# Due times in a list scheduler, and three GpSimd operations moved to VectorE, in a streaming-encoder layer

## The chip, the cores and the metric

The kernel runs on one core of a Trainium2 chip. The metric is the device time of one execution in microseconds (us). A core has engines with instruction queues of their own: TensorE (PE; its weight loads are listed as PEld), VectorE (DVE), ScalarE (ACT), GpSimd (POOL), and SyncE (SP), which issues most of the DMA transfers. Each engine executes its queue in order; a semaphore makes an instruction wait for another engine or for a transfer, and what stands behind it on the same queue waits with it.

## The reference

One layer of a streaming encoder is applied to a prompt of 2048 frames and to 8 running streams of 16 new frames each (the "sample"), with shared weights. Cut to what matters:

```python
h = rms_norm(x, norm_g)
z = einsum("btd,de->bte", h, w_in)                 # 1024 -> 3584 columns
u_a, v_a, g_a, q, k, v, g_b = split(z)             # 512 columns each
y_a = u_a * spatial_gate(v_a, ...) * silu(g_a)     # 4 groups x 128, W_s lower-triangular in 128-chunks
q, k = rms_norm(q), rms_norm(k)                    # per 64-wide half, 4 heads x 2 halves
# per head: two score maps; ALiBi distance; block-causal mask for the prompt
s = q @ k.T / 8 - slope[h] * abs(q_pos - k_pos)
a = softmax(s[half 0]) - lam * softmax(s[half 1])
o = rms_norm(a @ v, subln_g) * (1 - lam_init)
y_b = o * silu(g_b)
y = x + concat(y_a, y_b) @ w_out
```

For the sample, keys and values are the 1024 cached frames of each stream followed by its 16 new ones. Besides y, the new keys and values and the sample's `v_a` are outputs.

## The kernel before

**Number form.** All products are in fp32r. An operand that needs more precision is held as two parts: the high part is a rounded copy (`act.copy` on ACT), the low part is source minus high part. `split` does both; its argument `lo_eng` chooses the engine of the low part (DVE unless POOL is named). `mm3` multiplies two split operands with three matmuls. Every matmul is recorded on line 394 and every transpose on line 398, so tiles tell them apart; `split` has ACT on line 459 and the low part on line 460.

**Stages.**

1. *Projection* (`p1_pools`, `stream`). Tiles of 128 frames are normalized and transposed (`x_tp`, `xT`). Blocks of 256 columns of `w_in` are loaded in eight pieces (`load_w`: `wraw` by SP, scaled on ACT into `w`'s high part on line 626, the low part on DVE on line 627), and `project` accumulates `acc`. The kinds of block are `qk`, `v`, `ug` (gate and u) and `vg` (v and gate). `vg_group` normalizes `v_a` (`vn`, line 724; `vhl`), and makes the attention's gate: `gate` gives `sg` on DVE (line 690), and line 715 multiplies it by the constant `subg` into `gb`, which goes to the scratch `g_scr`.
2. *Sample attention*, woven into the projection. `sample_scores` loads cached keys (`skraw`), transposes and splits them (`skT`), and multiplies them with a block-diagonal query (`qbd`) into `sS`. Of `sS`, one half of the partitions is copied by ACT into `slo` (line 1104), line 1105 adds the distance `dist_s` to it, and DVE adds the other half and takes the running maximum into `sp` (line 1106). `sample_values` loads values (`svraw`, a ring of two buffers), splits them into `sv` (ring of two; low part on POOL), and accumulates `sO`.
3. *Prompt attention*. Frames 0 to 1023 (`attention_a`) are woven into the projection; 1024 to 2047 into the output projection. `score_steps` makes `S` and the exponentials `ex` (lines 889, 893, 905, 908, 909), `value_steps` transposes them (`a_tp`, `aT`) and accumulates `oT`. Values (`v_chunk`) are split with the low part on POOL.
4. *Output projection* (`out_stream`): `y_tp`, `yT`, `oo`, and the sum with x in `xo`.

**The order.** `weave` lays out program order: it takes steps of two generators in turn by estimated TensorE time. Then `Order(tc).run()`, a list scheduler of the kernel's own, fixes the order of each engine's queue. It replays the whole program on a clock. An instruction becomes ready when all those that it depends on have ended by that clock (`cost` gives to each a time to its result and a time that it holds its engine; `reach` and `SLACK`/`OTHER` are added for a result that goes to another engine; a transfer takes `FETCH` ns and more), and its buffers are free. For two-operand DVE work and POOL work, which `port` marks, it also keeps DVE and POOL out of each other's way. Whenever an engine is free, it takes among the ready instructions the one that comes first in program order:

```python
heapq.heappush((turn if port[i] else now_)[e], i)
...
i = heapq.heappop(turn[e])
```

SP's transfers are put in order the same way. The result is tied down as same-engine dependencies; on the chip the queues then run by semaphores alone.

Of the kernel before, what the change touches and what calls it, by code (L numbers as in the profile page):

```python
# [16 lines left out]
ALU = mybir.AluOpType  # L17
# [42 lines left out]
class Order:  # L60
# [4 lines left out]
    PE, ACT, DVE, POOL, SP = (mybir.EngineType.PE, mybir.EngineType.Activation, mybir.EngineType.DVE,  # L65
                              mybir.EngineType.Pool, mybir.EngineType.SP)

    SLACK = {PE: 180.0, SP: 300.0}
    OTHER, FETCH = 50.0, 2300.0

    class Node:
        def __init__(self, ins, idx):
# [115 lines left out]
    def cost(self, n):  # L188

        kind = type(n.ins).__name__[4:]  # L190
        size = max([math.prod([k for s, k in a.ap[1:]]) for a in n.reads + n.writes] or [1])
        accum = len(n.writes) > 1
        if n.dma:
            return 0.0, 560.0 if n.engine == self.POOL else 400.0
        if n.engine == self.PE:
            size = math.prod([k for s, k in n.writes[0].ap[1:]])
            t = 109.0 if size <= P else 4 + 0.4455 * size
            return t + 165, t
        if n.engine == self.ACT:
            t = 165 + 0.83 * size if kind == "TensorCopy" else 205 + 0.835 * size  # L200
            return (t + 190, t + 90) if accum else (t, t - 105)
        if n.engine == self.DVE:
            t = {"TensorTensor": 160 + 1.04 * size, "TensorReduce": 160 + 1.03 * size, "Memset": 100 + 0.5 * size,
                 "Reciprocal": 162.0}.get(kind, 205 + 1.04 * size)
            if size == 1:
                return (270.0, 190.0) if kind == "TensorScalarPtr" else (165.0, 90.0)
            if kind == "TensorScalarPtr" and not n.ins.is_scalar_tensor_tensor:
                t = 170 + 0.56 * size
            return (t + 100, t - 40) if accum else (t, t - 85)
        if kind == "Memset":  # L210
            return 100 + 0.83 * size, 100 + 0.83 * size
        if "pow" in str(n.ins):
            return 300 + 200.0 * size, 250 + 200.0 * size
        t = 190 + 2.16 * size if kind == "TensorTensor" else 195 + 1.1 * size
        return t, t - 50

    def port(self, n):

# [7 lines left out]
        large = math.prod([k for s, k in n.writes[0].ap[1:]]) >= 512 and type(n.ins).__name__ == "InstTensorScalarPtr"  # L226
        return int(len(wide) > 1 or (len(wide) == 1 and large and not psum))

    def run(self):
        N = self.nodes  # L230
        reach = {self.PE: 54.0, self.POOL: 80.0, self.SP: 27.0}
        for n in N:
            n.wait = len(n.deps)
            for d in n.deps:
                N[d].after.append(n.idx)
# [17 lines left out]
        for g in self.gates:  # L253
            for i in g[1]:
                gate[i].append(g)
            for i in g[2]:
                N[i].wait += 1
        cost = [self.cost(n) for n in N]
        ready = [0.0] * len(N)
        left = {k: len(q) for k, q in self.queue.items()}  # L260
        users = {x: len(self.uses[x]) for x in self.tag}
# [51 lines left out]
        while left_over:  # L313
            t, e = None, None
            for x in free:
                lock = busy[2 if x == self.DVE else 1]
                for y in ((free[x],) if now_[x] else ()) + ((max(free[x], lock),) if turn[x] else ()) + (
                        (max(free[x], later[x][0][0]),) if later[x] else ()):
                    if t is None or y < t:
                        t, e = y, x  # L320
            while later[e] and later[e][0][0] <= t:
                i = heapq.heappop(later[e])[1]
                heapq.heappush((turn if port[i] else now_)[e], i)
            lock = busy[2 if e == self.DVE else 1]
            if turn[e] and lock <= t and (not now_[e] or turn[e][0] < now_[e][0]):
                i = heapq.heappop(turn[e])
            elif now_[e]:
                i = heapq.heappop(now_[e])
            else:
                continue  # L330
            left_over -= 1
            n = N[i]
            out[e].append(i)
            if n.dma:
                size = 4 * math.prod([k for s, k in n.writes[0].ap])
                dma = max(t + self.FETCH, dma) + max(size / 280, 60.0)
                end = dma + 200
            else:
                end = t + cost[i][0]
            free[e] = t + cost[i][1]  # L340
            if port[i]:
                busy[port[i]] = free[e]
            for j in n.after:
                b = N[j].engine
                if b == e and not n.dma and not N[j].dma:
                    r = free[e]
                else:
                    r = end + reach.get(b, 35.0) + (self.SLACK.get(b, self.OTHER) if b != e or n.dma else 0)
                ready[j] = max(ready[j], r)
                N[j].wait -= 1  # L350
                if not N[j].wait:
                    arrive(j)
            more = list(first[i])
            for g in gate[i]:
                g[0] -= 1
                if not g[0]:
                    more += g[2]
            for j in more:
                ready[j] = max(ready[j], t)
                N[j].wait -= 1  # L360
                if not N[j].wait:
                    arrive(j)
            for name in n.tiles:
                if name in users:
                    last[name] = max(last.get(name, 0.0), end + 35)
                    users[name] -= 1
                    if not users[name]:
                        taken.discard(slot[name])
                        freed[slot[name]] = last[name]
            while held and place():  # L370
                pass
# [7 lines left out]
def trunk_step_kernel(  # L379
# [97 lines left out]
    turn = {}  # L477
# [30 lines left out]
    def p1_pools(stage, at):  # L508
# [194 lines left out]
        def vg_group(h, tiles, w, loads):  # L703
# [5 lines left out]
            for k, (pr, load) in enumerate(zip(pairs(tiles), loads)):  # L709
                m = len(pr)  # L710
                acc = yield from project(pr, w, load)
                va = sbg.tile([P, 2, P], F32, name="va", tag="va")[:, :m]
                act.copy(va, acc[:, :, 0])
                s = gate(acc, m)
                pool.tensor_tensor(out=gb[:, 2 * k:2 * k + m], in0=s,  # L715
                                   in1=subg.unsqueeze(1).broadcast_to([P, m, P]), op=ALU.mult)
                if sample:
                    sp.dma_start(nsg[:, h * P:(h + 1) * P], va[:, 0])
                st = sb.tile([P, 2, 2], F32, name="vst", tag="vst")
                for i in range(m):  # L720
                    act.activation(vn[:, 2 * k + i], va[:, i], AF.Square, scale=ISQ128, accum_out=st[:, 0, i:i + 1])
                rstd(st[:, 1, :m], st[:, 0, :m])
                for i in range(m):
                    dve.scalar_tensor_tensor(out=vn[:, 2 * k + i], in0=va[:, i], scalar=st[:, 1, i:i + 1],
                                             in1=sgug[:, h], op0=ALU.mult, op1=ALU.mult)
# [333 lines left out]
    def sample_scores(sa, b, qkT, qbd, dist_s, res):  # L1059
# [12 lines left out]
        for u in units:  # L1072
# [19 lines left out]
            if pend:  # L1092
                ci_, h_, kT_, w_ = pend
                s = bank("sS", "sS")[:, :w_]
                for i in range(2):
                    g = h_ + i
                    for z in range(2):
                        pe.matmul(s, lhsT=qbd[:, g * P:(g + 1) * P], rhs=kT_[:, z, i, :w_],
                                  start=i == 0 and z == 0, stop=i == 1 and z == 1)
                cost += pe_time(4 * w_)  # L1100
                hp, x = h_ // 2, 256 * ci_
                rh, rl = [slice(64 * k, 64 * k + 64) for k in (hp, 1 - hp)]
                lo = los[rh, ci_ % 2, :w_]
                act.copy(lo, s[rl])  # L1104
                pool.tensor_tensor(out=lo, in0=lo, in1=dist_s[rh, x:x + w_], op=ALU.add)  # L1105
                dve.tensor_tensor_reduce(out=p[rh, x:x + w_], in0=s[rh], in1=lo, scale=1.0, scalar=prev[hp],
                                         op0=ALU.add, op1=ALU.max, accum_out=st[rh, ci_:ci_ + 1])
                prev[hp] = st[rh, ci_:ci_ + 1]
# [16 lines left out]
    def sample_values(sa, b, a):  # L1125
        bs = slice(b * QS, (b + 1) * QS)

        def load(kt):
            n = P if kt < 8 else QS
            raw = sa.tile([P, 512], F32, name="svraw", tag="svraw")[0:n]  # L1130
            sp.dma_start(raw, cv[b, kt * P:(kt + 1) * P] if kt < 8 else nvs[bs].rearrange("t h d -> t (h d)"))
            v = sa.tile([P, 2, 512], F32R, name="sv", tag="sv")[0:n]
            split(raw, v[:, 0], v[:, 1], pool)
            return v

        vs = [load(0), load(1)]
# [76 lines left out]
    with ExitStack() as left, ExitStack() as right:  # L1213
# [108 lines left out]
        x = 0  # L1322
# [63 lines left out]
```

## Time and profile before

| | |
|---|---|
| median of 3 runs | 1396.93 us (1396.93 to 1399.89) |
| the profiled execution | 1396.8 us, span 1395.0 us |
| granted TensorE clock, mean | 0.998 |
| busy share PE / PEld / DVE / ACT / POOL | 97 / 90 / 64 / 57 / 44 % |
| matmuls | 9892 |
| PE busy in the slice 0 to 50 us | 36.65 us |
| POOL, low part of `sv` (72 instructions) | 94.4 us |
| POOL, `slo` plus distance (64) | 50.0 us |
| POOL, `gb` (36) | 26.6 us |

A row of the groups gives the line, engine, operation, tiles written and read, shape and count; then busy time in us and the mean of one in ns; then the engine's idle time just before those instructions, and what ended it. In a row of a tile, the three numbers are minimum, median and maximum duration in ns. Overlapping records make busy time smaller than count times mean.

### The profile page before, as it was taken

How to read it: one execution, taken by the hardware profiler on the slowest of the kernel's cores; microseconds unless marked ns; L12 is line 12 of the kernel's file. 1: busy time of each engine (PE TensorE's matmuls, PEld its weight loads, DVE VectorE, ACT ScalarE, POOL GpSimd, SP SyncE). 2: the span in 40 equal slices, each digit the busy share in tenths (PEclk: the TensorE clock that was granted, in tenths of full speed). 3: DMA queues.
4: the chain of work that ended last, by engine and by line, in shares of the span. 5: the costliest groups of instructions: out<-in, count | busy, mean ns of one | idle time of the engine just before them, and what ended most of it. 6: DMA issues, size and time to landing. Idle time of an engine off the chain costs nothing. (4 is left out here: it accounts for less than half of the span.)

```text
span 1395.0 us, 27945 instructions
## 1 busy us (share of the span) xinstructions
PE 1355.2 (97%) x9892; PEld 1258.4 (90%) x9892; DVE 889.4 (64%) x2114; ACT 794.0 (57%) x1778; POOL 615.9 (44%) x796
## 2 busy tenths in 40 slices
PE   6999999999999999999999999999999999999998
PEld 5999999999999899999999999997788888888887
DVE  4433447765666684798887764324888887877721
ACT  5433347766565776677656553224676777676620
POOL 2261534646464565656625142023555545445400
PEclk9999999999999999999999999999999999999999
DMA  6623234544545576645533242235555444442323
GB/s 196 191 82 112 71 89 144 158 140 131 144 125 154 151 205 193 180 126 130 159 92 110 74 145 81 79 120 190 157 150 166 129 120 127 148 125 65 103 84 102
DMA packets 209244, 183.05 MB, mean 131 GB/s; under 512 B 21104, under 2 KB 167024, under 8 KB 209104
## 3 DMA queue, kind: packets, MB, share of 16 engines
q1 hardware_dynamic: 199280, 155.17, 37.9%
q0 software_dynamic: 9824, 26.09, 6.8%
q8 instruction: 78, 1.28, 0.4%
q14 instruction: 62, 0.51, 0.1%
HBM read 130.86 MB, written 42.47 MB: 124 GB/s over the span
## 5 line engine op out<-in xcount | busy, mean ns | idle before, releaser
L394 PE MATMUL acc<-w,xT 128*128 128x256 f32 x5376 | 715.2, 283 | 9.1 <-DVE w L627 3.1
L394 PEld LDWEIGHTS acc<-w,xT 128*128 128x128 f32 x5376 | 675.2, 190 | 23.2 <-DVE w L627 4.3
L394 PE MATMUL oo<-wo,yT 128*128 128x512 f32 x816 | 235.2, 401 | 1.0 <-ACT yT L459 1.0
L394 PE MATMUL S<-kT,qT 128*128 128x512 f32 (+3 forms) x688 | 184.9, 361 | 1.5 <-DMA qT<-qT 0.9
L893 ACT ACTIVATE ex<-ex,sst 128x128 f32<-128x128 f32 (+15 forms) x128 | 153.8, 1203 | 41.5 <-DVE sst L889 41.1
L394 PEld LDWEIGHTS oo<-wo,yT 128*128 128x128 f32 x816 | 146.1, 188 | 25.1 <-ACT yT L459 1.5
L394 PE MATMUL oT<-aT,v 128*128 128x256 f32 x864 | 154.6, 295 | 0.2
L627 DVE SCALAR_TENSOR_TENSOR w<-wraw,normg,w 128x256 fp32r<-128x256 f32 x224 | 119.3, 559 | 54.2 <-ACT w L626 52.9
L889 DVE CUSTOM_DVE_ANT_0 ex<-S,dist,sst 128x512 f32<-128x512 f32 (+2 forms) x192 | 123.6, 653 | 33.1 <-PE S L394 31.6
L626 ACT ACTIVATE w<-wraw,normg 128x256 fp32r<-128x256 f32 x220 | 104.3, 505 | 65.6 <-DMA wraw<-in_w_in_dram 49.1
L460 POOL TENSOR_TENSOR sv<-svraw,sv 128x512 fp32r<-128x512 f32 (+1 forms) x72 | 94.4, 1314 | 89.4 <-ACT sv L459 63.4
L394 PEld LDWEIGHTS oT<-aT,v 128*128 128x128 f32 x864 | 122.8, 190 | 6.0 <-DVE aT L460 0.8
L394 PEld LDWEIGHTS S<-kT,qT 128*128 128x128 f32 x688 | 111.8, 189 | 17.7 <-DVE sst L889 3.9
L459 ACT CAST aT<-a_tp 128x512 fp32r<-128x512 f32 (+1 forms) x144 | 79.8, 560 | 79.7 <-PE a_tp L398 78.8
L460 DVE TENSOR_TENSOR aT<-a_tp,aT 128x512 fp32r<-128x512 f32 (+1 forms) x144 | 94.0, 658 | 23.1 <-ACT aT L459 22.2
L398 PE MATMUL a_tp<-ident,ex 128*128 128x128 f32 x544 | 89.9, 276 | 5.5 <-DVE ex L905 4.1
L889 DVE CUSTOM_DVE_ANT_0 ex<-S,dist 128x512 f32<-128x512 f32 (+3 forms) x128 | 78.7, 629 | 21.0 <-PE S L394 14.8
L398 PEld LDWEIGHTS a_tp<-ident,ex 128*128 128x128 f32 x544 | 64.0, 141 | 21.2 <-issue 5.2
L1105 POOL TENSOR_TENSOR slo<-slo,dist_s 64x256 f32<-64x256 f32 (+1 forms) x64 | 50.0, 781 | 68.6 <-ACT slo L1104 63.1
L909 POOL TENSOR_TENSOR ex<-ex 128x1024 f32<-128x1024 f32 (+4 forms) x32 | 58.5, 1849 | 20.9 <-ACT ex L908 20.8
L905 DVE SCALAR_TENSOR_TENSOR ex<-ex,sst 128x1024 f32<-128x1024 f32 (+4 forms) x64 | 63.6, 1000 | 1.3
L715 POOL TENSOR_TENSOR gb<-sg,subg 128x256 f32<-128x256 f32 (+1 forms) x36 | 26.6, 738 | 82.0 <-DVE sg L690 81.7
(144 smaller groups left out, 1931.0 us busy)
## 6 DMA issues: line engine op xcount, KB each, us to landing
wraw<-in_w_in_dram SPq DMA_DIRECT2D x160, 128.0 KB, 2.7
skraw<-in_cache_k_dram SPq DMA_DIRECT2D x64, 256.0 KB, 3.1
svraw<-in_cache_v_dram SPq DMA_DIRECT2D x64, 256.0 KB, 3.0
kT<-k_scr POOLq DMA_DIRECT2D x20, 512.0 KB, 5.7
vraw<-out_dram SPq DMA_DIRECT2D x36, 256.0 KB, 2.9
y<-y_scr SPq DMA_DIRECT2D x34, 256.0 KB, 3.1
out_dram<-xo SPq DMA_DIRECT2D x34, 256.0 KB, 2.0
wraw<-in_w_in_dram SPq DMA_DIRECT2D x128, 64.0 KB, 2.5
```

The source lines that it names most:

```text
L394: pe.last = nc.tensor.matmul(*a, **k).ins
L398: pe.last = nc.tensor.transpose(*a, **k).ins
L459: act.copy(hi, src)
L460: (lo_eng or dve).tensor_tensor(out=lo, in0=src, in1=f(hi), op=ALU.subtract)
L626: act.activation(w[:, 0], r, AF.Copy, scale=normg[:, kc:kc + 1])
L627: dve.scalar_tensor_tensor(out=w[:, 1], in0=r, scalar=normg[:, kc:kc + 1], in1=f(w[:, 0]), op0=ALU.mult, op1=ALU.subtract)
L715: pool.tensor_tensor(out=gb[:, 2 * k:2 * k + m], in0=s, in1=subg.unsqueeze(1).broadcast_to([P, m, P]), op=ALU.mult)
L889: dve.tensor_tensor_reduce(out=ex[c][:, a:b], in0=s, in1=dist[:, off + a:off + b], scale=SLOPES[h], scalar=prev[c], op0=ALU.add, op1=ALU.m ...
L893: act.activation(ex[c][:, :w], ex[c][:, :w], AF.Exp, bias=prev[c], scale=-1.0, accum_out=st[:, c, 6:7])
L905: dve.scalar_tensor_tensor(out=p0, in0=p1, scalar=st[:, 1, 7:8], in1=p0, op0=ALU.mult, op1=ALU.add)
L909: pool.tensor_tensor(out=p0, in0=p1, in1=p0, op=ALU.add)
L1105: pool.tensor_tensor(out=lo, in0=lo, in1=dist_s[rh, x:x + w_], op=ALU.add)
```

## The change

Two things are edited.

*The scheduler.* A new function `deadlines` gives every instruction a due time. It lays the PE instructions end to end in program order by their cost; a PE instruction's due time is its place on that axis, and it stays so. Any other instruction starts with the axis value at its place in the program plus `LATE` (15 us). Then, from the last to the first, its due time is lowered to that of each instruction that depends on it (or that needs its buffer next), less its own duration and the reach to the other engine. The heaps hold `(rank, index)` instead of the index, so the ready instruction that is due first goes first. Four figures of the clock change: PE's `SLACK`, `FETCH`, POOL's time to a result, and a dependent instruction on DVE, POOL or ACT now becomes ready only at the end of the one before it plus a gap (`same`), not when the engine is free.

*Three operations.* The low part of `sv`, the distance added to `slo`, and the product `gb` are done by DVE; POOL did them.

```diff
-    SLACK = {PE: 180.0, SP: 300.0}
-    OTHER, FETCH = 50.0, 2300.0
+    SLACK = {PE: 250.0, SP: 300.0}
+    OTHER, FETCH, LATE = 50.0, 2500.0, 15000.0
...
         t = 190 + 2.16 * size if kind == "TensorTensor" else 195 + 1.1 * size
-        return t, t - 50
+        return t, t + 70
...
+    def deadlines(self, cost, reach):
+
+        N, t, when = self.nodes, 0.0, []
+        for n in N:
+            when.append(t)
+            if n.engine == self.PE:
+                t += cost[n.idx][1]
+        due = [x if n.engine == self.PE else x + self.LATE for n, x in zip(N, when)]
+        then = [set(n.after) for n in N]
+        for k, q in self.queue.items():
+            for a, b in zip(q, q[self.bufs[k]:]):
+                for i in self.uses[a]:
+                    then[i].add(self.uses[b][0])
+        for n in reversed(N):
+            end = self.FETCH + 600 if n.dma else cost[n.idx][0]
+            for j in then[n.idx]:
+                if j > n.idx:
+                    due[n.idx] = min(due[n.idx], due[j] - end - reach.get(N[j].engine, 35.0))
+        return [w if n.engine == self.PE else d for n, w, d in zip(N, when, due)]
...
+        same = {self.DVE: 25.0, self.POOL: 80.0, self.ACT: 20.0}
...
+        rank = self.deadlines(cost, reach)
...
-                heapq.heappush((turn if port[i] else now_)[e], i)
+                heapq.heappush((turn if port[i] else now_)[e], (rank[i], i))
...
-                i = heapq.heappop(turn[e])
+                i = heapq.heappop(turn[e])[1]
...
-                    r = free[e]
+                    r = max(free[e], end + same[e]) if e in same else free[e]
...
-                pool.tensor_tensor(out=gb[:, 2 * k:2 * k + m], in0=s,
+                dve.tensor_tensor(out=gb[:, 2 * k:2 * k + m], in0=s,
...
-                pool.tensor_tensor(out=lo, in0=lo, in1=dist_s[rh, x:x + w_], op=ALU.add)
+                dve.tensor_tensor(out=lo, in0=lo, in1=dist_s[rh, x:x + w_], op=ALU.add)
...
-            split(raw, v[:, 0], v[:, 1], pool)
+            split(raw, v[:, 0], v[:, 1])
```

More of the change, by code (lines that the diff above doesn't have):

```diff
@@ L322, in run @@
                 i = heapq.heappop(later[e])[1]
-                heapq.heappush((turn if port[i] else now_)[e], i)
+                heapq.heappush((turn if port[i] else now_)[e], (rank[i], i))
             lock = busy[2 if e == self.DVE else 1]
             if turn[e] and lock <= t and (not now_[e] or turn[e][0] < now_[e][0]):
-                i = heapq.heappop(turn[e])
+                i = heapq.heappop(turn[e])[1]
             elif now_[e]:
-                i = heapq.heappop(now_[e])
+                i = heapq.heappop(now_[e])[1]
             else:
```

## The prediction

> **What bounds the kernel now.** I read the page's head and its groups first, then the busy time by stage, then what TensorE (PE) waited for.
>
> ```profile
> span 1395.0 us, 27945 instructions
> PE 1355.2 (97%) x9892; PEld 1258.4 (90%) x9892; DVE 889.4 (64%) x2114; ACT 794.0 (57%) x1778; POOL 615.9 (44%) x796
> L394 PE MATMUL acc<-w,xT 128*128 128x256 f32 x5376 | 715.2, 283 | 9.1 <-DVE w L627 3.1
> ```
>
> TensorE is the bound, and only 1395.0 − 1355.2 = 39.8 us of it lie open. Its busy time hides more: one matmul is recorded as 283 ns long, but 430 of them in 50 us (below, 100 to 150) are 116 ns apart. So I measure loss by rate as well. Columns: stretch, length, busy us (instructions) of PE, weight load, VectorE (DVE), ScalarE (ACT), GpSimd (POOL), granted clock, DMA share, GB/s.
>
> ```profile
> 0.00:50.00 50.00, 36.65 (x258) 33.67 (x258) 22.49 (x48) 25.45 (x49) 10.58 (x28) 0.97 0.74 220
> 100.00:150.00 50.00, 50.00 (x430) 50.00 (x429) 14.53 (x26) 15.53 (x31) 14.85 (x15) 1.00 0.33 95
> 200.00:560.00 360.00, 352.14 (x2770) 335.32 (x2769) 232.26 (x528) 236.01 (x571) 190.59 (x220) 1.00 0.53 154
> 250.00:300.00 50.00, 50.00 (x392) 47.85 (x391) 37.23 (x81) 34.54 (x81) 27.75 (x31) 1.00 0.48 140
> 350.00:400.00 50.00, 49.62 (x401) 48.07 (x401) 32.29 (x74) 29.76 (x72) 24.63 (x27) 1.00 0.54 146
> 550.00:800.00 250.00, 246.08 (x1952) 237.97 (x1951) 201.73 (x520) 159.50 (x423) 125.95 (x200) 1.00 0.45 123
> 700.00:750.00 50.00, 50.00 (x404) 48.70 (x404) 39.07 (x103) 30.34 (x84) 16.43 (x33) 1.00 0.34 95
> 950.00:1100.00 150.00, 142.69 (x835) 120.36 (x834) 118.91 (x302) 101.92 (x194) 79.23 (x100) 0.99 0.50 148
> 1150.00:1200.00 50.00, 50.00 (x309) 42.71 (x308) 40.50 (x99) 34.97 (x60) 25.54 (x29) 1.00 0.43 129
> ```
>
> 200 to 560 us holds the sample attention, woven into projections. It runs 2770 matmuls; at the rate of its best stretch (401 in 50 us) they need 2770 / 8.02 = 345.4 us, so 14.6 us are lost there. The prompt's first attention, 550 to 800: 1952 at 404 per 50 us need 241.6, 8.4 lost. The second attention's start, 950 to 1100: 835 at 309 per 50 us need 135.1, 14.9 lost (its mix of shapes differs somewhat, so this is an upper figure). The first 50 us have 13.35 us open. These four pools are all that a better order can draw on. Next, what PE waited for over the whole run (total us, times, longest):
>
> ```profile
> PE x_tp L398 <- DVE x L583: 8.7, 2, 8.3
> PE a_tp L398 <- DVE ex L905: 4.1, 3, 1.8
> PE acc L394 <- DVE w L627: 3.1, 3, 1.7
> PE sO L394 <- ACT sv L459: 3.0, 5, 1.2
> PE sO L394 <- POOL sv L460: 1.7, 2, 0.9
> ```
>
> Both sO waits are the sample values' high and low part: 4.7 of the 360.00 − 352.14 = 7.9 us open in the sample stage, 60%. The 8.7 us are the wait for the first x.
>
> **The moved instructions.** In the sample stage, by group (count | busy us, mean ns | engine idle before); the POOL rows move, the DVE rows stay:
>
> ```profile
> L460 POOL TENSOR_TENSOR sv<-svraw,sv 128x512 fp32r<-128x512 f32 x62 | 81.4, 1314 | 72.8 <-ACT sv L459 46.8 <-issue 7.4 <-PE sk_tp L398 4.8
> L460 POOL TENSOR_TENSOR sv<-svraw,sv 16x512 fp32r<-16x512 f32 x8 | 10.5, 1317 | 3.8 <-ACT sv L459 3.8
> L1105 POOL TENSOR_TENSOR slo<-slo,dist_s 64x256 f32<-64x256 f32 x48 | 37.1, 773 | 61.1 <-ACT slo L1104 56.2 <-DVE w L627 4.1
> L1105 POOL TENSOR_TENSOR slo<-slo,dist_s 64x272 f32<-64x272 f32 x16 | 12.9, 804 | 7.5 <-ACT slo L1104 6.9
> L715 POOL TENSOR_TENSOR gb<-sg,subg 128x256 f32<-128x256 f32 x16 | 12.5, 780 | 8.8 <-DVE sg L690 8.7
> L460 DVE TENSOR_TENSOR saT<-sa_tp,saT 128x256 fp32r<-128x256 f32 x16 | 6.7, 421 | 3.3 <-ACT saT L459 3.1
> L627 DVE SCALAR_TENSOR_TENSOR w<-wraw,normg,w 128x256 fp32r<-128x256 f32 x72 | 44.4, 640 | 11.8 <-ACT w L626 11.4
> L724 DVE SCALAR_TENSOR_TENSOR vn<-va,vst,sgug 128x128 f32<-128x128 f32 x36 | 19.5, 570 | 7.6 <-POOL vst L467 7.6
> L460 DVE TENSOR_TENSOR qbd<-qkT,qbd 64x32 fp32r<-64x32 f32 x32 | 12.9, 402 | 2.6 <-ACT qbd L459 1.9
> ```
>
> POOL loses 81.4 + 10.5 + 37.1 + 12.9 + 12.5 = 154.4 of its 190.6 us in this stage. Minimum, median and maximum of those DVE lines and of one more over the run:
>
> ```profile
> L627 DVE SCALAR_TENSOR_TENSOR w<-wraw,normg,w x224: 462/480/1523, 8.6 to 920.3; 128x256 fp32r<-128x256 f32 x112
> L724 DVE SCALAR_TENSOR_TENSOR vn<-va,vst,sgug x68: 332/347/1548, 233.3 to 921.7; 128x128 f32<-128x128 f32 x68
> L460 DVE TENSOR_TENSOR qbd<-qkT,qbd x32: 173/189/1308, 203.9 to 473.8; 64x32 fp32r<-64x32 f32 x32
> L460 DVE TENSOR_TENSOR vhl<-vn,vhl x20: 279/688/1179, 250.7 to 922.8; 128x512 fp32r<-128x512 f32 x16, 128x128 fp32r<-128x128 f32 x4
> ```
>
> vhl is the nearest row to the new sv: the same subtraction of two SBUF operands, 688 ns against 1314. Bounds: 688 and 1179. slo and gb have 256 columns: 421 (saT) to 480 (w); I take 421. Load added to DVE: 70 × 0.688 + 64 × 0.421 + 20 × 0.421 = 48.2 + 26.9 + 8.4 = 83.5 us. Load removed: w, vn and qbd, which read two SBUF operands, take 640, 570 and 402 ns in this stage against medians of 480, 347 and 189; the excess is 72 × 0.160 + 36 × 0.223 + 32 × 0.213 = 26.4 us, with maxima one POOL instruction above the minimum, and I put it down to POOL holding a read path that they need. With 154.4 of 190.6 us of POOL gone, 81% of it goes: 21.4 us. DVE then has 232.3 + 83.5 − 21.4 = 294 of 360 us, 82%. Does PE stand that? In 1150 to 1200 DVE is busy 40.5 of 50 us (81%), and PE has no gap. So the added load by itself costs nothing; without relief it would be 316 of 360.
>
> The Trainium skill ("SBUF — State Buffer", Who interferes with whom) says that a DVE instruction with two SBUF inputs contends with a GpSimd one that reads SBUF, and the loser blocks for all of it; the maxima above agree. By it the 26.4 us would shrink as taken, and the sum stays.
>
> What the move brings is in the sv chain. Its transfer can start only when a slot of svraw is free, which the low part ends:
>
> ```profile
> SPq L1131 <- POOL sv L460: 78.7, 40, 4.3
> POOL slo L1105 <- ACT slo L1104: 63.1, 32, 13.0
> POOL sv L460 <- ACT sv L459: 50.6, 30, 3.8
> DVE skT L460 <- ACT skT L459: 25.1, 27, 2.7
> 507.92 2.97 POOL L460 TENSOR_TENSOR sv<-svraw,sv 128x512 fp32r<-128x512 f32 x2
> 510.95 0.50 PE L394 MATMUL sO<-sv,saT 128*128 128x512 f32 x1 [0.94 <-POOL sv L460]
> ```
>
> (The first four are waits in 200 to 560, the last two a timeline.) Two low parts in a row held POOL 2.97 us, and PE stood 0.94 us for the second. At 0.69 each the pair takes 1.4. SP's queue stood 78.7 us for those slots, with later loads and stores behind it; each goes 0.6 us earlier. If 60% of the 14.6 us is this chain, 8.7 us could go; ACT's cast can still be late, so I take half of the pool: −7.3.
>
> The cost: the moved instructions wait for ACT, 63.1 and 50.6 us on POOL, where little stood behind them. On DVE's queue the w, skT and sg operations stand behind, and PE behind those. The list issues one only when its own clock calls it ready, so only misjudged waits count. Low end 0. High end: DVE waited 25.1 us for 64 skT (0.39 each); 154 × 0.39 = 60 us, and 316 + 60 = 376 of 360 us, 16 over. Near the low end, as in 1150 to 1200; I take a tenth, +1.6. The other 16 gb (after 560) add 16 × 0.421 = 6.7 us to DVE beside matmuls; only a store reads them: 0, and at most 6.7 if DVE had no room. No DMA is added; the gb store leaves as early.
>
> **The order.** PE's rank stays program order. DVE, ACT, POOL and SP now take, among ready instructions, the one due first (a leaf: 15 us after its place) instead of the first written. No instruction is added for it. The new SLACK, FETCH, POOL cost and same-engine latency only shift the list's clock. Below nothing is possible: a deferred split or load may come late. I take a quarter of the 8.4 us at 550 to 800 (−2.1), since DVE there mixes urgent transposes with weights prepared blocks ahead, and a fifth of the 14.9 at 950 to 1100 (−3.0): its L905 waits (4.1) come from long DVE operations beside POOL's v, which stays. After 1100, 0: PE has few gaps. Bounds for all three: +6 (their sum reversed) and half the pools, −12. At the start:
>
> ```profile
> 11.80 2.50 SPq L531 DMA_DIRECT2D bias_s<-in_sgu_b_dram  x4
> 14.89 1.30 SPq L612 DMA_DIRECT2D wraw<-in_w_in_dram  x3
> 17.82 0.39 PE L394 MATMUL acc<-w,xT 128*128 128x256 f32 x1 [1.79 <-ACT w L626]
> 1391.31 0.69 DVE L1312 TENSOR_TENSOR xo<-oo,xo 128x512 f32<-128x512 f32 x1 [4.91 <-PE oo L394]
> ```
>
> Weights are fetched behind four loads of a constant used much later; up to 1.79 us, I take −1.0. The tail after the last matmul (1391 to 1395) stays.
>
> Sum: −7.3 + 1.6 − 2.1 − 3.0 − 1.0 = −11.8. The profiled execution took 1396.8 us (1.8 beside its span), 0.1 under the median of the three runs: 1396.8 − 11.8 = **1385.0**.
>
> **Rivals.** *B, the order finds nearly all:* 80% of 14.6, 60% of 8.4 and of 14.9, 2 at the start: 11.7 + 5.0 + 8.9 + 2 = 27.6, 1369. For it: the waits are short and scattered, as misordering makes them. Against: 3.0 us of the sO waits are for ACT, which gets no lighter.
> *C, the move is neutral:* DVE's two-input instructions lock POOL out in turn, and DVE's own queue delays the sv part by what its shorter duration saves. Only the order's 6.1 us remain: 1391. Against: POOL keeps just 36 us here, so there is little left to collide. The Trainium skill ("Perfetto Trace Analysis", Optimizing Scalar/DVE Operations) says that moving work between these two might not help because of that port; the 26.4 us of excess show the port costing DVE time.
> *D, no change:* list and chip disagree by as much as the due times set right; the waits change name: 1396.
> *E, slower: DVE becomes the sample stage's bound.* Its place is 250 to 300: 37.2 busy; by its share of the stage, 83.5 × 50/360 = 11.6 more makes 48.8 of 50. It decides once the relief fails or new waits exceed (360 − 294) / 154 = 0.43 us each. Price at the high end: +16, less the order's 6.1: 1407. For it: ACT is late 0.39 us on average already for skT. Against: the stretch 1150 to 1200.
>
> **How the numbers follow.** Chances: the forecast 0.42 (1378 to 1390), B 0.14, C 0.14, D 0.10, E 0.20. About 0.2% (2.8 us) is what a measurement of this kernel can tell from no change. Faster: 0.42 + 0.14 + 0.14 = 0.70; same 0.10; slower 0.20. The range runs from B's middle to near E's, leaving out about half of each, 0.17: 1370 to 1405.
>
> **What the changed profile would show.** Right: in the sample stage POOL near 36 us and DVE near 294; w, vn and qbd means near their medians; sv low parts at 0.69; sO waits under 2 us; over 7.85 matmuls per us there. For the order: fewer a_tp and acc waits before 800 and at 950 to 1100, wraw ahead of bias_s. Wrong: DVE over 330 us in the stage, PE waiting for DVE skT or w there (E); DVE means unchanged (C); or gaps of the same sum under other names (D).

## The result, and the profile after

The changed kernel takes 1381.11 us (median of 4 runs, 1380.71 to 1381.83) against 1396.93: a ratio of 0.9885, 95% interval [0.9868, 0.9902], 15.8 us less. The forecast was 1385.0 in a range of 1370 to 1405. In the sets below, two executions at a granted clock of 0.75 and 0.78, where all others had 0.99 or more, are left out of the ratios.

The head of the page after, and one group. In the changed kernel the helper lines have moved by 22: 394, 398, 460, 627, 905 of before are 416, 420, 482, 649, 927.

```profile
span 1380.1 us, 27913 instructions
PE 1347.1 (98%) x9892; PEld 1260.5 (91%) x9892; DVE 925.7 (67%) x2286; ACT 791.2 (57%) x1778; POOL 452.1 (33%) x624
L416 PE MATMUL acc<-w,xT 128*128 128x256 f32 x5376 | 715.3, 283 | 3.6 <-DVE w L649 1.8
```

POOL gave 172 instructions and 163.8 us to DVE, whose busy time grew by only 36.3. PE's open time is 33.0 us, 6.8 less; the other 8.1 us of the shorter span were inside what the profile counts as PE's busy time, for the same 9892 matmuls. Busy time by stretch:

```profile
0.00:50.00 50.00, 34.70 (x242) 33.52 (x243) 23.87 (x55) 25.21 (x49) 10.83 (x29) 0.93 0.71 220
200.00:560.00 360.00, 355.34 (x2805) 340.11 (x2804) 277.78 (x685) 238.06 (x575) 40.45 (x70) 1.00 0.52 154
550.00:800.00 250.00, 245.36 (x1965) 238.60 (x1965) 199.39 (x520) 157.31 (x420) 121.18 (x190) 1.00 0.46 123
950.00:1100.00 150.00, 146.63 (x883) 124.88 (x882) 124.37 (x323) 109.62 (x208) 83.30 (x106) 1.00 0.55 159
```

The first 50 us run 242 matmuls where before ran 258: the start is worse. The sample stage runs 35 more, 550 to 800 13 more, 950 to 1100 48 more. Such counts are rough: a second profile of the changed kernel has 2817 in the sample stage where this one has 2805, and a stage that starts earlier puts other work into the window. A milestone is safer: the last projection matmul starts at (last number before the semicolon) in the kernel before, and then in the changed one:

```profile
L394 PE MATMUL acc<-w,xT x5376: 274/280/582, 10.2 to 942.5; 128*128 128x256 f32 x200
```

```profile
L416 PE MATMUL acc<-w,xT x5376: 274/280/580, 11.0 to 937.5; 128*128 128x256 f32 x200
```

Of the 14.9 us of span, 5.0 are gained by the end of the projection and 9.9 behind it, where none of the three moved operations runs. What PE waited for, after:

```profile
PE x_tp L420 <- DVE x L605: 9.3, 2, 7.2
PE sO L416 <- ACT sv L481: 3.2, 2, 2.3
PE x_tp L420 <- DVE neglam L474: 3.1, 1, 3.1
PE a_tp L420 <- DVE ex L927: 0.9, 2, 0.6
PE sO L416 <- DVE sv L482: 0.2, 1, 0.2
```

The sO waits are 3.4 us where they were 4.7; the a_tp waits for the combination of the two score maps (line 905, now 927) fell from 4.1 to 0.9; a wait that carries the name of a small constant on DVE (`neglam`) is new.

### The profile page after: what moved, and what is told of

Read it like the earlier page. It is cut to its first block, busy times and chain, and to the rows that moved or that the text cites. A ratio compares the mean times of both kernels' runs of the same rounds, so it can differ in the third digit from the quotient of the medians.

```text
span 1380.1 us, 27913 instructions
## 1 busy us (share of the span) xinstructions
PE 1347.1 (98%) x9892; PEld 1260.5 (91%) x9892; DVE 925.7 (67%) x2286; ACT 791.2 (57%) x1778; POOL 452.1 (33%) x624
## 3 DMA queue, kind: packets, MB, share of 16 engines
q8 instruction: 78, 1.28, 0.4%
## 4 chain that ended last, share of the span: by engine, by line
PE 89%; DMA 4%; ACT 3%; DVE 2%; issue 1%; SPq 1%; POOL 0%; ACTq 0%; DVEq 0%
PE acc L416 44%; PE oo L416 13%; PE S L416 9%; PE oT L416 7%; PE a_tp L420 4%; PE sS L416 2%; PE sk_tp L420 2%; PE sO L416 2%; PE y_tp L420 1%; DMA svraw<-in_cache_v_dram 1%; PE mix L416 1%; PE x_tp L420 1%; DMA wraw<-in_w_in_dram 1%; PE k_tp L420 1%; ACT sa L1142 1%
## 5 line engine op out<-in xcount | busy, mean ns | idle before, releaser
L416 PE MATMUL oo<-wo,yT 128*128 128x512 f32 x816 | 231.7, 400 | 1.3 <-ACT yT L481 1.3
L416 PEld LDWEIGHTS oo<-wo,yT 128*128 128x128 f32 x816 | 146.5, 188 | 26.6 <-ACT yT L481 1.8
L416 PE MATMUL oT<-aT,v 128*128 128x256 f32 x864 | 150.7, 293 | 0.2 <-ACT aT L481 0.2
L649 DVE SCALAR_TENSOR_TENSOR w<-wraw,normg,w 128x256 fp32r<-128x256 f32 x224 | 105.5, 496 | 57.9 <-ACT w L648 56.5
L911 DVE CUSTOM_DVE_ANT_0 ex<-S,dist 128x512 f32<-128x512 f32 (+3 forms) x128 | 79.2, 629 | 21.4 <-PE S L416 16.5
L488 POOL TENSOR_SCALAR vst<-vst 128x2 f32<-128x2 f32 (+1 forms) x36 | 9.0, 250 | 257.3 <-ACT vn L743 256.4
L482 DVE TENSOR_TENSOR sv<-svraw,sv 128x512 fp32r<-128x512 f32 (+1 forms) x72 | 50.3, 700 | 22.4 <-ACT sv L481 21.6
L481 ACT CAST sv<-svraw 128x512 fp32r<-128x512 f32 (+1 forms) x72 | 44.3, 618 | 32.6 <-DMA svraw<-in_cache_v_dram 15.0
```

Of the source, the lines that this page charges most:

```text
L416: pe.last = nc.tensor.matmul(*a, **k).ins
L481: act.copy(hi, src)
L482: (lo_eng or dve).tensor_tensor(out=lo, in0=src, in1=f(hi), op=ALU.subtract)
L488: pool.tensor_scalar(out=ms, in0=ms, scalar1=1.0, scalar2=EPS, op0=ALU.mult, op1=ALU.add)
L649: dve.scalar_tensor_tensor(out=w[:, 1], in0=r, scalar=normg[:, kc:kc + 1], in1=f(w[:, 0]), op0=ALU.mult, op1=ALU.subtract)
L911: dve.tensor_tensor_reduce(out=ex[c][:, a:b], in0=s, in1=dist[:, off + a:off + b], scale=SLOPES[h], scalar=prev[c], op0=ALU.add, op1=ALU.m ...
```

## The experiments

The theories: **M**, the forecast's, in which the move brings the larger part in the sample stage; **O**, in which the order alone brings the gain behind the projection. A second set then asked which part of the scheduler's edit does it. All twelve runs in one table; "end" is the start of the last projection matmul, "rest" the span from there, "a_tp" PE's waits of a_tp for line 905 or 927, "open" the time from 945 to 1100 in which PE is not busy, all in us and from the profiled execution, which can lie some 4 us off the median (1390.0 against 1394.17 with the four clock figures back).

| kernel | median us | ratio to before | end | rest | a_tp | open |
|---|---|---|---|---|---|---|
| before | 1394.5 to 1396.9 (by set) | 1 | 942.5 | 452.5 | 4.1 | 7.3 |
| changed | 1381.11 | 0.9885 [0.9868, 0.9902] | 937.5 | 442.6 | 0.9 | 3.4 |
| changed, again | 1379.78 | 0.9892 [0.9874, 0.9910] | 935.5 | 444.0 | 1.1 | 3.4 |
| order alone | 1384.49 | 0.9929 [0.9907, 0.9952] | 939.0 | 442.4 | 1.0 | 3.4 |
| move alone | 1397.30 | 1.0020 [1.0007, 1.0034] | 943.0 | 451.1 | 3.0 | 5.9 |
| four clock figures back | 1394.17 | 0.9998 [0.9981, 1.0015] | 939.4 | 448.8 | 4.9 | 7.3 |
| rank back to program order | 1395.68 | 1.0009 [0.9994, 1.0025] | 945.1 | 448.9 | 3.8 | 7.0 |
| same-engine gap back | 1396.89 | 1.0019 [1.0008, 1.0031] | 946.3 | 452.4 | 4.8 | 7.0 |
| TensorE slack back | 1384.57 | 0.9936 [0.9914, 0.9958] | 938.1 | 443.8 | 1.3 | 3.4 |
| FETCH back | 1384.06 | 0.9920 [0.9901, 0.9939] | 939.3 | 443.2 | 1.8 | 4.1 |
| POOL's hold time back | 1381.55 | 0.9913 [0.9891, 0.9935] | 939.4 | 444.4 | 1.0 | 3.2 |
| other three back | 1388.68 | 0.9948 [0.9928, 0.9967] | 938.3 | 444.6 | 1.5 | 3.7 |
| release of transfers | 1385.79 | 0.9928 [0.9911, 0.9945] | 935.4 | 447.5 | 2.6 | 6.8 |
| release at the start | 1380.78 | 0.9892 [0.9873, 0.9911] | 935.5 | 444.0 | 1.3 | 3.4 |

**Order alone** (the changed kernel, with the three operations on POOL).

```diff
-                dve.tensor_tensor(out=gb[:, 2 * k:2 * k + m], in0=s,
+                pool.tensor_tensor(out=gb[:, 2 * k:2 * k + m], in0=s,
...
-                dve.tensor_tensor(out=lo, in0=lo, in1=dist_s[rh, x:x + w_], op=ALU.add)
+                pool.tensor_tensor(out=lo, in0=lo, in1=dist_s[rh, x:x + w_], op=ALU.add)
...
-            split(raw, v[:, 0], v[:, 1])
+            split(raw, v[:, 0], v[:, 1], pool)
```

> The scheduler of the changed kernel (due times and new clock figures); the three operations stay on POOL as before. Theory O (the order alone brings the gain behind the projection): 1386 to 1388, the last projection matmul at 941 to 943 us as before (942.5), and nearly the whole 9.9 us that the changed kernel gained after that point kept. Theory M (the forecast: the move brings the larger part): about 1391, the order being worth some 6 us. If the move also helped the second attention: over 1393.

0.9929, or some 10 us, with the rest at 442.4 us as in the changed kernel: theory O in that, and not M. The median, 1384.49, is below the range of both, and the projection ends at 939.0, 3.5 us before the 942.5 that O took to stay, so the order also gains there. Busy time from 200 to 560:

```profile
200.00:560.00 360.00, 354.87 (x2804) 339.49 (x2804) 227.25 (x531) 237.80 (x574) 193.22 (x220) 1.00 0.52 153
```

The sample stage runs as many matmuls as in the changed kernel (2804 against 2805) with the 193 us of POOL work still in place.

**Move alone** (the kernel before, with the three operations on DVE): the last three pairs of the change's diff, and nothing else.

```diff
-                pool.tensor_tensor(out=lo, in0=lo, in1=dist_s[rh, x:x + w_], op=ALU.add)
+                dve.tensor_tensor(out=lo, in0=lo, in1=dist_s[rh, x:x + w_], op=ALU.add)
...
```

> The old scheduler (program order, old clock figures); the three operations on VectorE. Theory O: 1391 to 1393, last projection matmul near 938, and the second attention as before (some 452 us from there to the end). Theory M: 1387 to 1390. If VectorE's in-order queue suffers without due times (rival E): 1398 or more, with VectorE over 300 us busy between 200 and 560 us.

Not faster, 0.2% slower. It falls into no theory's range: O and M expected at most 1393 us, E at least 1398 with DVE over 300 us busy, and it takes 1397.30 with 277. The projection ends at 943.0, where O expected some 938. The relief of DVE that the forecast counted on is there in full. Busy time of the stage, then groups in it, then PE's waits over the run:

```profile
200.00:560.00 360.00, 353.50 (x2776) 336.20 (x2776) 277.06 (x684) 237.66 (x571) 39.83 (x68) 1.00 0.52 153
```

```profile
L627 DVE SCALAR_TENSOR_TENSOR w<-wraw,normg,w 128x256 fp32r<-128x256 f32 x72 | 32.8, 478 | 4.4 <-ACT w L626 4.2
L724 DVE SCALAR_TENSOR_TENSOR vn<-va,vst,sgug 128x128 f32<-128x128 f32 x36 | 11.2, 346 | 1.1 <-POOL vst L467 0.8
L460 DVE TENSOR_TENSOR qbd<-qkT,qbd 64x32 fp32r<-64x32 f32 x32 | 5.9, 183 | 1.0 <-ACT qbd L459 0.5
```

```profile
PE sO L394 <- ACT sv L459: 3.0, 7, 0.8
PE sk_tp L398 <- DVE skT L460: 1.7, 4, 0.8
```

w, vn and qbd are at 478, 346 and 183 ns where they were 640, 570 and 402. Yet the stage runs 2776 matmuls, 6 more than before, which is less than two profiles of one kernel differ by. The sO waits for POOL (1.7) went, and waits of sk_tp for DVE (1.7) came. So the 26 us that contention cost DVE, and the 0.6 us by which each sv part got shorter, were hidden: the move is neutral as long as the order is the old one. The Trainium skill says ("Perfetto Trace Analysis", Optimizing Scalar/DVE Operations) that work moved between these two might not help; this run agrees on the time, though not because the port ate the gain, since DVE got the contended time of these three groups back.

**Changed, again**, to set the move's share on top of the order apart.

> The changed kernel once more, beside the two below on one chip, to set the move's share apart: with the order alone it was 0.9929 of the kernel before [0.9907, 0.9952], with both 0.9885 [0.9868, 0.9902]. If the move is worth some 0.4% on top of the order: ratio 0.987 to 0.991. If that was a difference between chips: 0.991 to 0.994.

0.9892, against 0.9929 for the order alone: the move is then worth about 0.4% (some 5 us). The first measurement's interval lies clear of the order's, the second's overlaps it by a little (0.9910 and 0.9907). Where in the stage the move's 5 us come from, no run shows: PE's sO waits are 3.4 us with the move and 1.0 with the order alone.

**Four clock figures back**, and **rank back**: the changed kernel with SLACK, FETCH, POOL's figure and the same-engine gap of before; and with the place in program order as the rank.

```diff
-        rank = self.deadlines(cost, reach)
+        rank = list(range(len(N)))
```

> The changed kernel with its due times and its move, but the four figures of the scheduler's clock (TensorE slack, FETCH, POOL's time to a result, same-engine gap) as before. If the rank by due time makes the order's gain: 1381 to 1384. If the clock's figures make it: 1387 to 1391.

> The changed kernel with its move and its new clock figures, but the rank is the place in program order again. If the rank by due time makes the order's gain: 1388 to 1392, near the move alone. If the clock's figures make it: 1382 to 1385.

Both lose all of it (0.9998 and 1.0009). Neither expectation allowed for that: beside the move, due times and clock each are worth nothing alone, and 1% together.

**One figure back at a time**, in the changed kernel. POOL's figure is the second of the two that `cost` returns, the time that an instruction holds its engine, and not the time to its result:

```diff
-    SLACK = {PE: 250.0, SP: 300.0}
+    SLACK = {PE: 180.0, SP: 300.0}
...
-    OTHER, FETCH, LATE = 50.0, 2500.0, 15000.0
+    OTHER, FETCH, LATE = 50.0, 2300.0, 15000.0
...
-        return t, t + 70
+        return t, t - 50
...
-                    r = max(free[e], end + same[e]) if e in same else free[e]
+                    r = free[e]
```

> The changed kernel, one clock figure back: TensorE slack 180 instead of 250. The four together back cost all of the gain (1394 against 1381). Theory K (TensorE's slack is what the due times need, because a matmul planned too close to its operand stalls): 1388 or more, with more and shorter waits of TensorE. Theories Q and G (POOL's time, same-engine gap): 1380 to 1384. Theory Z (no single figure, each reshuffle costs a few us): 1384 to 1388 in all four runs of this set.

> The changed kernel, FETCH back to 2300 from 2500. No theory gives it the gain: transfers mostly land early enough; 1380 to 1384. Over 1387 would say that transfers planned 200 ns early stall the queues (waits for DMA on ACT or TensorE up). Theory Z: 1384 to 1388.

> The changed kernel, POOL's time that it holds its engine and the shared read path back to 50 ns under its duration (70 ns over it in the changed kernel). Theory Q (the figure keeps DVE's two-operand instructions, L927 above all, from being planned into a POOL instruction that is still running): 1387 or more, and the mean of L927 at 945 to 1100 us up from 987 towards 1118 ns, with waits of a_tp for it. Theories K and G: 1380 to 1384. Theory Z: 1384 to 1388.

> The changed kernel, without the same-engine gap: a dependent instruction on DVE, POOL or ACT counts as ready when its engine is free. Theory G (the gap lets the list put other work between two dependent ones, which fills the engines that feed TensorE): 1387 or more, and idle time of DVE up between 945 and 1100. Theories K and Q: 1380 to 1384. Theory Z: 1384 to 1388.

Theory G: without the same-engine gap the kernel is at 1.0019, with nothing of the gain left. The granted clock does not make this: its mean over the executions was 0.994 without the gap, 0.996 in the changed kernel again and 0.997 in the kernel before; 0.2% of 1380 us would be 3 of the 17 between the first two. Beside the changed kernel on the same chip (1379.78) slack, FETCH and POOL's figure cost 4.8, 4.3 and 1.8 us; only for the slack do the intervals lie apart. Theory K fell (1388 or more expected), and Q: with POOL's old figure line 927 stayed short (its mean at 945 to 1100 was 943 ns) and its waits at 1.0 us. Theory Z's range holds for slack and FETCH, but not for all four. These three kernels run 2787, 2757 and 2770 matmuls from 200 to 560, where before ran 2770, and end 10 us and more sooner: the stage in which the gain falls changes from list to list.

What a changed order does can be seen at one place, the first long combination of the second attention. Without the gap, DVE, POOL and PE (timeline: start us, length us, instruction, [idle before]):

```profile
976.90 0.16 DVE L919 RECIPROCAL sst<-sst 128x1 f32<-128x1 f32 x1 [2.35 <-ACT ex L915]
977.10 0.28 DVE L920 TENSOR_SCALAR sst<-sst,neglam 128x1 f32<-128x1 f32 x1
977.40 0.42 DVE L485 SCALAR_TENSOR_TENSOR qT<-q_tp,qT 64x256 fp32r<-64x256 f32 x1
977.86 2.21 DVE L927 SCALAR_TENSOR_TENSOR ex<-ex,sst 128x1024 f32<-128x1024 f32 x1
977.72 1.26 POOL L482 TENSOR_TENSOR v<-vraw,v 128x512 fp32r<-128x512 f32 x1 [0.57 <-ACT v L481]
980.21 0.63 PE L420 MATMUL a_tp<-ident,ex 128*128 128x128 f32 x4 [3.02 <-DVE ex L927]
```

The same place in the changed kernel:

```profile
968.65 0.16 DVE L919 RECIPROCAL sst<-sst 128x1 f32<-128x1 f32 x1 [0.93 <-ACT ex L915]
968.85 0.27 DVE L920 TENSOR_SCALAR sst<-sst,neglam 128x1 f32<-128x1 f32 x1
969.15 0.43 DVE L485 SCALAR_TENSOR_TENSOR qT<-q_tp,qT 64x256 fp32r<-64x256 f32 x1
969.61 1.28 DVE L927 SCALAR_TENSOR_TENSOR ex<-ex,sst 128x1024 f32<-128x1024 f32 x1
969.88 0.58 POOL L878 DMA_DIRECT2D qT<-qT  x1 [1.23 <-DVE qT L485]
970.49 1.54 POOL L482 TENSOR_TENSOR v<-vraw,v 128x512 fp32r<-128x512 f32 x1
970.03 0.41 PE L420 MATMUL q_tp<-ident,qraw 128*128 128x128 f32 x2 [1.30 <-DMA qraw<-q_scr]
971.04 1.06 PE L420 MATMUL a_tp<-ident,ex 128*128 128x128 f32 x8 [0.60 <-DVE ex L927]
```

Without the gap, POOL's low part of v starts 0.14 us before line 927, which reads two SBUF operands, and that instruction takes 2.21 us; PE stands 3.02. In the changed kernel POOL first issues a transfer, v comes 0.88 us after line 927 has begun, and it takes 1.28; PE stands 0.60 for it, but 1.30 before that for the transfer of `qraw`. So the loss at this place is 3.02 − 1.90 = 1.12 us, and not the 2.42 by which the wait with the name of line 927 shrank. The Trainium skill ("SBUF — State Buffer", Who interferes with whom) has the loser of that port blocked for the whole instruction: 2.21 − 1.28 = 0.93 us, against 1.12 of v's 1.26 us that were left to run, so the trace comes near it.

What the gap corrects can be read here too. Line 920 needs the result of line 919 and starts 0.20 us after it in both kernels. The list's `cost` has line 919 hold DVE for 90 ns and give its result after 165; without the gap the list counts 90 ns from the one to the other, with it 165 + 25 = 190. Up to line 927 the costs of the three instructions ahead of it add up to 90 + 190 + 386 = 666 ns without the gap and 766 with it, an estimate from the code, where the chip took 0.96 us. Without the gap DVE is thus some 0.3 us late by the list's clock, and POOL's v starts 0.14 us ahead of line 927. That this error let v in is argued, not shown: no trace has the list's own times, with the gap 0.2 us of error stay, and in the changed kernel v also stood behind a store on POOL's queue.

The table fits in part. The five kernels at 1394 us or more have 3.0 to 4.9 us of a_tp waits for this line and 5.9 to 7.3 us of open PE time, the others but one 0.9 to 1.8 and 3.2 to 4.1; the one is the release below. But with the rank back the waits are 3.8 us, and at both of them the line takes 1.28 us: there it came late, and was not long. Between the gap-back and the changed kernel the open time differs by 3.6 us, of some 16 in the medians. The rest lies in waits under 1 us that change place from kernel to kernel and in PE's busy time; that the same cause makes them is not shown.

**Other three back**: due times, gap and move, with the old SLACK, FETCH and POOL figure.

> Due times, the same-engine gap and the move; TensorE slack, FETCH and POOL's time as before. Theory G (due times need a clock that knows the latency between dependent instructions of one engine, and little else): 1381 to 1387. If the other three figures are needed as well: over 1390.

0.9948: the gap with the due times brings about half; the other three figures bring the other half, 8.9 us (1388.68 against 1379.78), and singly they cost 10.9 in sum. The median is 1.7 us over the range of theory G and under the 1390 of its rival.

**The start.** Two kernels hold back transfers that nobody needs yet; the second keeps the rule to those due in the first 60 us:

```diff
-        ready = [0.0] * len(N)
+        ready = [max(0.0, rank[n.idx] - 15000.0) if n.dma else 0.0 for n in N]
...
# the second kernel:
-        ready = [0.0] * len(N)
+        ready = [max(0.0, rank[n.idx] - 15000.0) if n.dma and rank[n.idx] < 60000.0 else 0.0 for n in N]
```

> The changed kernel, with one edit in the list: a transfer is not ready before 15 us ahead of its due time, so that the constants leave SP's queue behind the first frames and weights. The changed kernel runs 242 matmuls in the first 50 us where the kernel before runs 258. Theory S (the constants' transfers and DVE's small operations on them, queued ahead of the frames, hold the start): 1376 to 1379, 260 to 275 matmuls in the first 50 us. Rival (the start is bound by the transfers' volume itself): 1380 to 1382, about 242 matmuls.

> As the release run, but the release holds only for transfers due in the first 60 us of the list's axis, so that the order after the start is the changed kernel's but for a few lines. That run gained at the start (259 matmuls in 50 us against 242) and lost at 950 to 1100 (885 against 907 in 945 to 1100). If the start gain is real and carries to the end, 17 matmuls of 0.116 us are 2.0 us: 1377 to 1379, ratio 0.986 to 0.988. Rival (what is gained at the start is given back where the next wait stands, in the sample stage): 1380 to 1382.

The first runs 259 matmuls in 50 us, one short of theory S's range, but its time missed that range by 7 us. Its start gain does not last: it runs 2787 matmuls in the sample stage against 2805 and 2817, and ends the projection at 935.4, where the changed kernel has 937.5 and 935.5. In the second attention it loses more (rest 447.5), where line 927 is long again (up to 2.2 us; its waits are 2.6). The second keeps the rest at 444.0 but did not bring the start about: 240 matmuls, 0.9892, no better than the changed kernel. So it does not test whether a start gain would carry to the end. Its SP queue, and ACT's wait for the fourth frame tile:

```profile
11.91 0.43 SPq L1064 DMA_DIRECT2D dist_s<-in_c_dist_s_dram  x1
12.39 2.94 SPq L593 DMA_DIRECT2D x<-in_x_prompt_dram  x4
22.19 1.06 ACT L600 ACTIVATE xsq<-x 128x1024 bf16<-128x1024 f32 x1 [4.45 <-DMA x<-in_x_prompt_dram]
```

and in the first kernel:

```profile
11.53 1.37 SPq L593 DMA_DIRECT2D x<-in_x_prompt_dram  x2
18.76 1.06 ACT L600 ACTIVATE xsq<-x 128x1024 bf16<-128x1024 f32 x1 [2.31 <-DMA x<-in_x_prompt_dram]
```

The limit at 60 us lets out what is due later, and three such transfers stand ahead of the frame here: `dist_s`, a constant of 520 KB, and two of the four `x`, which are frame tiles of 512 KB that ACT does not read before 189.5 us. By the trace these land at 18.24, 19.53 and 20.81 us and the fourth frame tile at 22.09, so that ACT starts on it 3.4 us later than in the first kernel. What stands ahead of the frames thus moves the start, and nothing measured here beats the changed kernel.

## Why the prediction was right or wrong, point by point

The total was right (−15.8 against −11.8), in part by luck: the largest term did not come by its mechanism, and the order alone brought some 10 us where 6.1 were forecast.

- *The sample values' chain, −7.3: this step failed.* It gave 60% of the stage's lost time to the two waits that carry the tile's name and let the shorter chain win half. Alone the move wins nothing there (6 matmuls, 0.8 us) and costs 0.2% in all, and the stage's gain is there with the order alone. On top of the new order the move is worth about 5 us, near the −5.7 of gain and new waits together, but not by those waits: sO waits are 3.4 us with it (forecast under 2) and 1.0 without. The cause of these 5 us stays open. The stage's rate is 2805 / 360 = 7.79 per us, short of the 7.85 that was to show. A wait's name says what came last, not what would be won if it came earlier.
- *DVE's load and relief.* Right in kind: 277.8 us busy in the stage (forecast 294, which took 21.4 us of relief where w, vn and qbd gave 26.6, and added durations that overlap by their ends), POOL 40.5 (36), w, vn and qbd fully at their medians (479, 344 and 186 ns). The instruction prices were right: sv 687 ns (688), slo 416 and gb 422 (421). PE did not feel DVE at 77%; rival E did not come.
- *The new waits, +1.6:* small, as taken; sk_tp's 1.7 us for skT in the move alone is one.
- *550 to 800, −2.1:* 13 more matmuls at 8.08 per us, 1.6 us: near it, as far as a fixed window tells.
- *950 to 1100, −3.0, and nothing after 1100: this term was mis-sized.* From the end of the projection on, 9.9 us were won. Behind 1100 us the kernel before had 1686 matmuls left and the changed one 1616; at 309 in 50 us these 70 are 11.3 us, so by this estimate some 6 of the 9.9 came up to 1100 and some 4 behind it. The forecast read the L905 waits as long DVE instructions beside POOL's v, which stays, and so as out of the order's reach. But the order sets how long such an instruction takes (2.21 or 1.28 us, by who starts first), and when it comes.
- *The start, −1.0: wrong sign.* The weights did go ahead of `bias_s`, but the first 50 us run 16 matmuls fewer: 16 × 0.116 = 1.9 us lost. The changed kernel puts four loads of `keep` ahead of the fourth frame tile, which reaches ACT no earlier than before (20.73 against 20.79 us), and PE stands 3.1 us for it. `neglam` only gives this wait its name: DVE scales the tile from 22.83 us on, as soon as POOL's factor is ready at 22.79. Which change on the queue cost the start was not taken apart.
- *"The new clock figures only shift the list's clock", taken at 0: the largest omission.* Without the same-engine gap the due times are worth nothing.
- *The rivals.* C's outcome holds for the move alone, but not its reason, whose sign was DVE means unchanged: they fell. D, list and chip out of step, fits due times on the old clock (1394.17). B and E did not come.

## What to carry to other kernels

A list scheduler is as good as its clock: better priorities brought nothing until the clock held a dependent instruction on the same engine back to the result of the one before, and not to the engine. Where two engines exclude each other, a lead of 0.14 us cost the other 0.93, so check whether the plan's order of starts is the chip's. When a wait shrinks, count the whole time that the bound engine stands at that place: here 1.12 us were won where the named wait fell by 2.42. And price a shorter chain by what the bound engine would do next: 26 us of contention on an engine with a third of its time free were worth nothing by themselves.

## What the runs showed of the hardware that was not expected

Taking 151 us of POOL work out of one stage (190.6 to 39.8 us busy, 200 to 560, in the move alone) gave DVE's contending instructions their full speed (640 to 478 ns, 570 to 346, 402 to 183) with no gain in time. On DVE an instruction that needs the result of the one before it started 0.04 us after that one's end (line 920 behind line 919, 968.81 to 968.85), where independent ones overlap: five w parts of 0.48 us in a row took 2.06 us in the changed kernel, 0.08 less for each that follows. Transfers on the SP queue landed in the order of issue at the start, those of 512 KB some 1.3 us apart (19.53, 20.81, 22.09 us), so three that were not needed yet made a frame tile 3.4 us late.
